# Keys and values through one wide product, and new places for tiles in SBUF, in a two-block transformer kernel

## The chip, the cores and the metric

The kernel runs on one core of one Trainium2 chip. The metric is the device time of one execution in microseconds (us); the kernel before takes 1009.96 us, the median of three runs (1009.23 to 1010.29). [...]

## The reference

The input is one sequence of 256 tokens with 1024 features, in fp32. The first block is a mixer with four branches (a short convolution, stick-breaking attention, an RWKV recurrence and a spatial gate), then a feed-forward with a short convolution. The second block has two layers; each has attention to a memory of 256 tokens, and a wide feed-forward. The change concerns the keys and values. Cut to that:

```python
def rmsnorm(x, g):
    y = x * lax.rsqrt(jnp.mean(x * x, axis=-1, keepdims=True) + EPS)
    return y * g

for l in range(2):
    if l == 1:                                   # layer 1: keys and values of the tokens
        kv = rmsnorm(h, kv_norm) @ w_kv          # (256, 1024) @ (1024, 512)
        k_shared = rmsnorm(kv[..., :256].reshape(B, S, 4, 64), k_norm)
        v_shared = kv[..., 256:].reshape(B, S, 4, 64)
    ...
    mkv = rmsnorm(mem, mem_norm[l]) @ w_mem_kv[l]   # both layers: keys and values of the memory
    mk = rmsnorm(mkv[..., :256].reshape(B, 256, 4, 64), mem_k_norm[l])
    mv = mkv[..., 256:].reshape(B, 256, 4, 64)
    mem_out = memory_attention(mqh, mk, mv)
    h = h + concat([main_out, mem_out]) @ w_out[l]
    h = h + square(relu(rmsnorm(h, norm_mlp[l]) @ w_up[l])) @ w_down[l]
```

There are thus three products for keys and values: the memory's for layer 0 and for layer 1, and the tokens' for layer 1. The keys are normalised head by head (4 heads of 64).

## The kernel before

All large products are done as three products of fp32r halves: each operand x is split into a high half h and a low half l, and `mm3` (L207) issues h·h, h·l and l·h into one accumulator in PSUM. A matmul here has a stationary operand (128 columns, loaded by LDWEIGHTS) and a moving operand (256 or 512 columns). A row `mm<-a,wh` of the profile names the output, then the moving and the stationary operand.

- `load_split` (L195) loads 512 KB of weights through SP's queue into a tile `raw`; ACT rounds it to `wh` (L203), DVE subtracts to get `wl` (L204). The tiles have four buffers each, of 1024 fp32 (4096 bytes a partition).
- `fm_part` (L254) gives an output with features on the partitions: weights stationary, activations moving, 256 columns (all tokens). `tm_part` (L262) gives an output with tokens on the partitions: activations stationary, 256 weight columns moving. Both are called narrow below. `wide_block` (L320) is as `tm_part`, with 512 weight columns moving, and is called wide. The up-projections of the last two feed-forwards (`fm_blocks`, L277) alternate: a matmul of 512 columns (both halves of the activation moving over `wh`), then one of 256 columns (the high half over `wl`).
- `tick()` steps generators that stand `beside` the main stream, so that small work (transposes, norms) comes between its pieces; `finish` runs one to its end. The scheduler then fixes each engine's order when the program is built; engines wait for each other by semaphores, and TensorE takes its matmuls in the order in which they stand.
- Keys before: `memory_keys` (L905), `memory_values` (L912) and L1441 to L1452 make keys features-first with `fm_part` and values tokens-first with `tm_part`, 48 narrow matmuls each. `scaled_keys` (L847) squares on ACT; `normed_keys` (L862) sums the squares by head with four fp32 matmuls of 2 columns (`head_sums`, `ssq`), takes the power -1/2 on GpSimd (`power`, L393), widens the factors on DVE (`rkx`, L440), spreads them over the features with four fp32 matmuls of 128 columns (`spread_heads`) and multiplies on DVE.
- Features of the first block's output for its feed-forward (`normalised_features`, L1095) are transposed beside `memory_values(1)`; the feed-forward's 22 up blocks follow (L1118).

Where tiles lie. The pools place tiles one after another, so a tile of a few bytes shifts what comes after it. In the built program, taking the byte at which the moving and the stationary operand start, modulo 256, the split matmuls stand so:

| split matmuls before | same remainder | stationary 64 further | moving 64 further | other |
|---|---|---|---|---|
| narrow, 2890 | 2624 | 48 (values of memory, layer 1) | 48 (keys of memory, layer 1) | 170 |
| wide, 2312 | 2096 | 24 (`yrw`) | 0 | 192 (`y`, both layers of block two) |

The 170 are the layer-0 memory products (96), the pool weights (42) and the band products (32).

Of the kernel before, what the change touches and what calls it, by code (L numbers as in the profile page):

```python
# [112 lines left out]
def build(tc, I, out):  # L113
# [345 lines left out]
    def load_const(p, key):  # L459
        t = p.tile([P, CARR[key].shape[1]], CDT[key], name=nm(key), tag=key)  # L460
# [33 lines left out]
    def mt(shape, name, dt=F32, tag=None, bufs=1):  # L494
        return m1.tile(shape, dt, name=nm(name), tag=tag or name, bufs=bufs)
# [351 lines left out]
    def scaled_keys(dst, z, gain, f):  # L847

        sq = scr([P, T], "ssq", f)
        S.activation(out=sq, in_=z, func=AF.Square)  # L850
        S.mul(dst, z, gain)
        return sq

# [8 lines left out]
    def normed_keys(dst, sq, f, m):  # L862

        yield
        r = scr([P, 4], "rk4", f)
        head_factor(r, head_sums(sq, f)[:, 0:4], m, f)
        yield
        wide = scr([P, 4, 64], "rkx", f)
        widen_heads(wide, r)
        yield  # L870
        tt(dst, dst, spread_heads(wide, 2, f))
# [33 lines left out]
    def memory_keys(l):  # L905
        o = halves(fm_block(I["w_mkv"][l, 0], hm[l]))
        return [scaled_keys(mkv[l][0][:, j], o[j], mem_gain[:, l : l + 1], "B") for j in range(2)]

    def memory_keys_norm(l, sqs):
        return together(*(normed_keys(mkv[l][0][:, j], sqs[j], "B", mmem) for j in range(2)))  # L910

    def memory_values(l):  # L912
        o = halves(tm_block(I["w_mkv"][l, 1], hm[l]))
        for j in range(2):
            S.mul(mkv[l][1][:, j], o[j], rmem[:, j : j + 1])
# [154 lines left out]
    ksq = memory_keys(0)  # L1070
    finish(mf)
    beside(memory_keys_norm(0, ksq))
# [10 lines left out]
    memory_values(0)  # L1083
    r = sums.mean()
    power(r)
    ksq = memory_keys(1)
    finish()
    xn = tok8()
    for j in range(2):
        late(S.mul(xn[:, j], x2[:, j], r[:, j : j + 1]))  # L1090
    xp = pair8()

    def normalised_features():
        yield from features(xn, range(KT), lambda k, z: split_scaled(xp[:, k], z, pvec("ffn_norm_g", k, k + 1)))

    nf = beside(normalised_features(), 0, 1.0)
    memory_values(1)
    finish(nf)
    beside(memory_keys_norm(1, ksq))
# [18 lines left out]
    for n in range(NFF):  # L1118
        o = halves(fm_block(I["w_up"][n], xp))
# [317 lines left out]
    snk = wa.tile([P, 12], F32, name="snk")  # L1437
    nc.gpsimd.dma_start(out=snk, in_=I["sinks"])
    kn = wa.tile([P, 2, T], F32, name="kn")
    mtok, rtok = wa.tile([P, 2], F32, name="mtok"), wa.tile([P, 2], F32, name="rtok")  # L1440
    o, vo = psum_mm(), psum_mm()  # L1441
    for a in (0, 4):
        if a:
            finish(tf)
            power(rtok, sums2.mean(mtok))
        fm_part(o, load_split(I["w_kv"][0][:, a : a + 4], 4), kvp[0], a, a + 4)
        tm_part(vo, load_split(I["w_kv"][1][:, a : a + 4], 4), kvp[0], a, a + 4)
    o, vo = halves(o), halves(vo)
# [138 lines left out]
```

## Time and profile before

| | |
|---|---|
| median of three runs | 1009.96 us |
| the profiled execution, its own time | 1010.36 us |
| its span on the chip | 1008.6 us |
| TensorE matmul busy | 998.1 us (99%) |
| VectorE, ScalarE, GpSimd busy | 690.8, 553.9, 142.1 us |
| DMA | 176.25 MB, 175 GB/s on average |

In the rows PE is TensorE (PEld its weight loads), DVE is VectorE, ACT is ScalarE, POOL is GpSimd. Matmuls are pipelined: the next one starts while the last still drains, so the durations of single matmuls add up to more than the span, and a group's "busy" counts a shared stretch once. What a matmul costs the stream is the distance from its start to the next one's start. "Mean ns" of a group is the duration of one, drain included.

### The profile page before, as it was taken

How to read it: one execution, taken by the hardware profiler on the slowest of the kernel's cores; microseconds unless marked ns; L12 is line 12 of the kernel's file. 1: busy time of each engine (PE TensorE's matmuls, PEld its weight loads, DVE VectorE, ACT ScalarE, POOL GpSimd, SP SyncE). 2: the span in 40 equal slices, each digit the busy share in tenths (PEclk: the TensorE clock that was granted, in tenths of full speed). 3: DMA queues.
4: the chain of work that ended last, by engine and by line, in shares of the span. 5: the costliest groups of instructions: out<-in, count | busy, mean ns of one | idle time of the engine just before them, and what ended most of it. 6: DMA issues, size and time to landing. Idle time of an engine off the chain costs nothing.

```text
span 1008.6 us, 16844 instructions
## 1 busy us (share of the span) xinstructions
PE 998.1 (99%) x6528; PEld 865.8 (86%) x6528; DVE 690.8 (68%) x1089; ACT 553.9 (55%) x965; POOL 142.1 (14%) x129
## 2 busy tenths in 40 slices
PE   9999999999999999999999999999999999999998
PEld 8999777788899999988987888888898668888886
DVE  6795477888558888855676777646468877776443
ACT  6754465365566655635665655535366466564331
POOL 0110001320000000001220344300021104443000
PEclk9999999999999999999999999999999999999999
DMA  8644533575466555555534555565562335555661
GB/s 285 226 148 136 177 116 114 162 250 192 169 209 195 182 180 188 188 188 187 174 123 145 188 184 188 186 196 187 189 226 88 105 104 182 188 185 189 197 209 64
DMA packets 50592, 176.25 MB, mean 175 GB/s; under 512 B 5776, under 2 KB 7056, under 8 KB 50128
## 3 DMA queue, kind: packets, MB, share of 16 engines
q1 hardware_dynamic: 50112, 174.38, 52.2%
q8 instruction: 51, 0.84, 0.3%
q10 hardware_dynamic: 288, 0.52, 0.1%
q0 software_dynamic: 112, 0.27, 0.1%
q14 instruction: 29, 0.24, 0.1%
HBM read 174.10 MB, written 1.05 MB: 174 GB/s over the span
## 4 chain that ended last, share of the span: by engine, by line
PE 91%; DVE 3%; ACT 2%; DMA 1%; issue 1%; SPq 0%; POOL 0%; ACTq 0%; DVEq 0%
PE mm L127 78%; PE ps L127 13%; DVE wl L204 1%; ACT wh L203 1%; DMA wlo<-in_lora 1%; DMA raw<-in_w_in 1%; DVE sc L360 0%; DVE mxs L1199 0%; DVE dd L363 0%; ACT uh L1349 0%; SPq L201 0%; ACT sc L1217 0%; DVE mxs L1205 0%; POOL var L393 0%; ACT sqw L409 0%
## 5 line engine op out<-in xcount | busy, mean ns | idle before, releaser
L204 DVE TENSOR_TENSOR wl<-raw,wh 128x1024 fp32r<-128x1024 f32 (+2 forms) x318 | 386.1, 1216 | 234.1 <-ACT wh L203 232.9
L203 ACT CAST wh<-raw 128x1024 fp32r<-128x1024 f32 (+2 forms) x318 | 328.4, 1034 | 349.1 <-PE mm L127 316.1
L127 PE MATMUL mm<-a,wh 128*128 128x256 f32 (+1 forms) x1520 | 363.6, 322 | 0.2 <-DVE a L363 0.2
L127 PE MATMUL mm<-a,wl 128*128 128x256 f32 x1008 | 283.9, 282 | 0.0
L127 PEld LDWEIGHTS mm<-a,wh 128*128 128x128 f32 x1520 | 252.9, 190 | 25.2 <-issue 0.7
L127 PEld LDWEIGHTS mm<-a,wl 128*128 128x128 f32 x1008 | 191.8, 190 | 0.1
L127 PE MATMUL mm<-wh,u 128*128 128x512 f32 x512 | 158.6, 389 | 0.0
L127 PE MATMUL mm<-wh,a 128*128 128x512 f32 (+1 forms) x512 | 144.7, 357 | 0.0
L127 PEld LDWEIGHTS mm<-wh,u 128*128 128x128 f32 x512 | 96.1, 188 | 20.1
L1274 POOL TENSOR_TENSOR u<-gate,u 128x256 fp32r<-128x256 f32 x64 | 84.4, 1320 | 160.0 <-ACT u L1273 160.0
L127 PEld LDWEIGHTS mm<-wh,a 128*128 128x128 f32 x512 | 90.8, 189 | 13.4 <-issue 0.3
L127 PE MATMUL mm<-wl,u 128*128 128x512 f32 x256 | 99.6, 389 | 0.0
L127 PE MATMUL mm<-wl,a 128*128 128x512 f32 (+1 forms) x256 | 89.7, 350 | 0.0
L127 PEld LDWEIGHTS mm<-wl,u 128*128 128x128 f32 x256 | 48.1, 188 | 9.7
L127 PE MATMUL mm<-wh,ff 128*128 128x512 f32 x176 | 54.9, 390 | 0.0
L127 PEld LDWEIGHTS mm<-wl,a 128*128 128x128 f32 x256 | 48.5, 189 | 5.4
L360 DVE SCALAR_TENSOR_TENSOR cv<-mm,pv,cv 128x255 f32<-128x255 f32 x88 | 42.2, 479 | 1.4
L127 PE MATMUL mm<-wh,y 128*128 128x512 f32 x112 | 38.6, 409 | 0.5 <-ACT y L352 0.5
L127 PEld LDWEIGHTS mm<-wh,ff 128*128 128x128 f32 x176 | 33.0, 188 | 6.8
L127 PE MATMUL mm<-wl,ff 128*128 128x512 f32 x88 | 34.3, 389 | 0.0
L360 DVE SCALAR_TENSOR_TENSOR gate<-gate 128x256 f32<-128x256 f32 x64 | 32.0, 502 | 2.0
L1149 POOL TENSOR_TENSOR a<-a,gfb 128x512 f32<-128x512 f32 x4 | 7.1, 1785 | 177.1 <-issue 149.8
(345 smaller groups left out, 1179.8 us busy)
## 6 DMA issues: line engine op xcount, KB each, us to landing
raw<-in_w_up SPq DMA_DIRECT2D x108, 512.0 KB, 3.6
raw<-in_w_dn SPq DMA_DIRECT2D x86, 512.0 KB, 3.3
raw<-in_w_in SPq DMA_DIRECT2D x36, 512.0 KB, 3.9
raw<-in_w_gate SPq DMA_DIRECT2D x32, 512.0 KB, 3.9
raw<-in_w_out SPq DMA_DIRECT2D x16, 512.0 KB, 3.8
raw<-in_outs SPq DMA_DIRECT2D x8, 512.0 KB, 4.0
raw<-in_w_mkv SPq DMA_DIRECT2D x8, 512.0 KB, 3.5
raw<-in_w_o SPq DMA_DIRECT2D x8, 512.0 KB, 4.2
```

The source lines that it names most:

```text
L127: ins = f(*a, **k)
L203: S.copy(wh[:, :m], raw[:, :m])
L204: V.tensor_tensor(out=wl[:, :m], in0=raw[:, :m], in1=wh[:, :m].bitcast(F32), op=ALU.subtract)
L360: return V.scalar_tensor_tensor(out=o, in0=a, scalar=sc, in1=b, op0=op0, op1=op1)
L1149: G.tensor_tensor(out=y3[:, j, c], in0=x3[:, j, c], in1=gfb[:, c], op=ALU.mult)
L1274: G.tensor_tensor(out=u.l[:, n], in0=sq, in1=u.h[:, n].bitcast(F32), op=ALU.subtract)
```

## The change

1. Keys and values come from one `wide_block` of 512 columns (256 of keys, 256 of values), tokens first, for all three products. `keys_values` copies the keys out of PSUM on ACT and scales the values there; DVE squares the keys and sums the squares by head (`tensor_reduce`). `normed_keys` forms the factor (DVE, GpSimd), multiplies on DVE, and TensorE transposes the normalised keys into features-first order (4 transposes for a product). The host packs the weights accordingly.
2. The first block's features are transposed in two parts: half of them beside the second memory product, half beside the start of the up blocks; the first two up blocks are done half by half (`up_blocks`).
3. Small tiles (`mt`, `load_const`, `snk`, `mtok`, `rtok`, `kss`) take whole lines of 256 bytes, and slots of `wh` and `wl` are 4352 bytes long instead of 4096.
4. In a slot, weights in pieces of fewer than 512 columns start 64 bytes in; wide ones start at 0.

| split matmuls after | same remainder mod 256 | stationary 64 further | moving 64 further |
|---|---|---|---|
| narrow, 2602 | 32 (band products) | 2330 | 240 |
| wide, 2456 | 1944 | 512 (up-projections of the last two feed-forwards) | 0 |

A slot is 17 × 256 bytes, so modulo 512 neighbouring slots differ by 256: of the wide matmuls with the same remainder modulo 256, half have the moving operand 256 bytes off modulo 512. Before, all 2096 agreed modulo 512.

```diff
     def load_split(src, kt, n=256, tag="w", bufs=4, size=1024, raw=None):
...
-        wh = wp.tile([P, size], F32R, name=nm("wh"), tag=tag + "h", bufs=bufs)
-        wl = wp.tile([P, size], F32R, name=nm("wl"), tag=tag + "l", bufs=bufs)
+        wh, wl = (wp.tile([P, size + 64], F32R, name=nm("w" + z), tag=tag + z, bufs=bufs) for z in "hl")
         m = kt * n
+        if n < 512:
+            wh, wl = wh[:, 16:], wl[:, 16:]
...
-    def wide_block(src, x, kt):
+    def wide_block(src, x, kt, half=None):
...
+            if half and a == kt // 2:
+                half()
...
     def load_const(p, key):
-        t = p.tile([P, CARR[key].shape[1]], CDT[key], name=nm(key), tag=key)
+        n = CARR[key].shape[1]
+        t = p.tile([P, (n + 63) // 64 * 64], CDT[key], name=nm(key), tag=key)[:, :n]
...
     def mt(shape, name, dt=F32, tag=None, bufs=1):
+        if shape[-1] < 64:
+            return m1.tile([P, 64], dt, name=nm(name), tag=tag or name, bufs=bufs)[:, : shape[-1]]
...
+    def keys_values(os_, mv, factor):
+        kz, ss = scr([P, 2 * T], "gate", bufs=4), scr([P, 8, 4], "kss", bufs=2)[:, :2]
+        for j, o in enumerate(os_):
+            with urgent():
+                S.copy(kz[:, j * T : j * T + T], o[:, :T])
+                S.mul(mv[:, j], o[:, T:], factor[:, j : j + 1])
+            sq = scr([P, T], "ssq", "B")
+            tt(sq, kz[:, j * T : j * T + T], kz[:, j * T : j * T + T])
+            V.tensor_reduce(out=ss[:, j], in_=sq.rearrange("p (h c) -> p h c", c=64), op=ALU.add, axis=AX.X)
+        return kz, ss
+
+    def normed_keys(dst, kz, ss, m, gain):
+        stt(ss, m.rearrange("p (a o) -> p a o", o=1).to_broadcast([P, 2, 4]), 64.0 * RMS_EPS, ss)
+        power(flat(ss))
+        for _ in range(2):
+            yield
+        heads = kz.rearrange("p (h c) -> p h c", c=64)
+        late(tt(heads, heads, flat(ss).rearrange("p (k o) -> p k o", o=1).to_broadcast([P, 8, 64])))
+        yield
+        o = psum("B")
+        for j in range(2):
+            for a in range(2):
+                TE.transpose(o[:, j * T + a * P : j * T + a * P + P], kz[:, a * T + j * P : a * T + j * P + P], ident)
+        S.mul(flat(dst), o, gain)
+        yield
...
+    def memory_kv(l):
+        kz, ss = keys_values(wide_block(I["w_mkv"][l], hm[l], KT), mkv[l][1], rmem)
+        return normed_keys(mkv[l][0], kz, ss, mmem, mem_gain[:, l : l + 1])
...
+    nf = beside(first_features(), 0, 1.0)
+    kf = memory_kv(1)
     finish()
...
+    beside(kf)
+    nf = beside(normalised_features(range(4, 8)), 0, 1.0)
...
+    def up_blocks():
+        os_ = [psum_mm(), psum_mm()]
+        for a in (0, 4):
+            if a:
+                finish(nf)
+            for n, o in enumerate(os_):
+                fm_part(o, load_split(I["w_up"][n][:, a : a + 4], 4), xp, a, a + 4)
+                if a:
+                    yield o
+        for n in range(2, NFF):
+            yield fm_block(I["w_up"][n], xp)
...
+    kz, ss = keys_values(wide_block(I["w_kv"], kvp[0], KT, ended), vt, rtok)
+    knf = beside(normed_keys(kn, kz, ss, mtok, swa_gain), 0, 1.0)
```

TensorE's order is the same in both programs up to the memory's first product. On TensorE at that place (`mem` the memory's split features, `mm` an accumulator, the row before it the end of the RWKV branch's output) stood before:

```order
L127 MATMUL ps_2714<-wl_2693,yrw_2357 128x512
L127 MATMUL ps_2714<-wh_2692,yrw_2358 128x512
L127 MATMUL mm_2724<-mem_2481,wh_2726 128x256
L127 MATMUL mm_2724<-mem_2483,wh_2726 128x256
L127 MATMUL mm_2724<-mem_2481,wl_2727 128x256
```

and on TensorE at the same place stands now:

```order
L127 MATMUL ps_2714<-wl_2693,yrw_2357 128x512
L127 MATMUL ps_2714<-wh_2692,yrw_2358 128x512
L127 MATMUL mm_2724<-wh_2727,mem_2481 128x512
L127 MATMUL mm_2724<-wl_2728,mem_2481 128x512
L127 MATMUL mm_2724<-wh_2727,mem_2483 128x512
```

Moving and stationary operand have changed places, and the moving one has 512 columns.

On TensorE after the tokens' keys and values, in layer 1 (`bq` the features of the query products that fill the time), the norm of the keys stood before as:

```order
L127 MATMUL mm_7846<-bq_6092,wl_7849 128x256
L127 MATMUL ps_7878<-cb_269,ssq_7836 128x2 x2
L127 MATMUL ps_7884<-cb_269,ssq_7839 128x2 x2
L127 MATMUL mm_7846<-bq_6092,wh_7890 128x256 x2
...
L127 MATMUL mm_7846<-bq_6092,wl_7891 128x256
L127 MATMUL ps_7923<-cb_269,rkx_7907 128x128 x2
L127 MATMUL ps_7927<-cb_269,rkx_7909 128x128 x2
L127 MATMUL mm_7939<-bq_6092,wh_7941 128x256 x2
```

and on TensorE there stands now (`gate` is the buffer of the keys), after 43 matmuls of the query product:

```order
L127 MATMUL mm_7684<-bq_5974,wl_7719 128x256
L127 MATMUL mm_7684<-bq_5974,wh_7718 128x256 x2
L127 MATMUL mm_7684<-bq_5974,wl_7719 128x256
L127 MATMUL ps_7748<-cb_269,gate_7671 128x128 x4
L127 MATMUL mm_7762<-bq_5974,wh_7764 128x256 x2
```

Eight fp32 matmuls have gone and four transposes have come.

On VectorE at the same place (`kss` the sums by head, `wl` the low half of weights to come), with what each waits for, stands now:

```order
L367 TENSOR_TENSOR ssq_7680<-gate_7671 128x256 [waits Activation_49]
L872 TENSOR_REDUCE kss_7672<-ssq_7675 128x4 [waits DVE_49]
L872 TENSOR_REDUCE kss_7672<-ssq_7680 128x4 [waits DVE_49]
L206 TENSOR_TENSOR wl_7807<-raw_7805,wh_7806 128x1024 [waits DMAHW5_49,PE_49,Activation_49]
L364 SCALAR_TENSOR_TENSOR kss_7672<-mtok,kss_7672 128x8 [waits DVE_49]
L367 TENSOR_TENSOR gate_7671<-gate_7671,kss_7672 128x512 [waits Pool_49]
L206 TENSOR_TENSOR wl_7910<-raw_7908,wh_7909 128x1024 [waits DMAHW6_49,PE_49,Activation_49]
```

A weight split stands between the sums and their use, and the multiplication waits for GpSimd with the next weight split behind it.

## Rows read from the trace of the kernel before

**Rows 1.** The page: TensorE's share, its granted clock, the chain of waits.
```profile
PE 998.1 (99%) x6528; PEld 865.8 (86%) x6528; DVE 690.8 (68%) x1089; ACT 553.9 (55%) x965; POOL 142.1 (14%) x129
...
PEclk9999999999999999999999999999999999999999
...
PE 91%; DVE 3%; ACT 2%; DMA 1%; issue 1%; SPq 0%; POOL 0%; ACTq 0%; DVEq 0%
```

**Rows 2.** TensorE's waits, longest of ten: engine, line, for whom, total, times, longest.
```profile
PE mm L127 <- DVE cold L485: 1.2, 1, 1.2
```

**Rows 3.** Groups by form, up blocks, 310 to 420 us: count, busy us, mean ns.
```profile
L127 PE MATMUL mm<-a,wh 128*128 128x256 f32 x613 | 110.4, 283 | 0.0
L127 PE MATMUL mm<-a,wl 128*128 128x256 f32 x306 | 86.6, 283 | 0.0
```

**Rows 4.** Groups by form, memory keys of layer 1, 281.5 to 286.5 us.
```profile
L127 PE MATMUL mm<-mem,wh 128*128 128x256 f32 x30 | 5.2, 276 | 0.0
```

**Rows 5.** Groups by form, memory values of layer 1, 287 to 290 us.
```profile
L127 PE MATMUL mm<-wh,mem 128*128 128x256 f32 x18 | 3.3, 281 | 0.0
```

**Rows 6.** Groups by form, the same product after four transposes, 290.9 to 291.6 us.
```profile
L127 PE MATMUL mm<-wh,mem 128*128 128x256 f32 x4 | 0.7, 277 | 0.0
```

**Rows 7.** Groups by form, up-projection of a last feed-forward, 570 to 640 us.
```profile
L127 PE MATMUL mm<-a,wh 128*128 128x512 f32 x199 | 70.4, 399 | 0.0
L127 PE MATMUL mm<-a,wl 128*128 128x256 f32 x198 | 55.6, 281 | 0.0
```

**Rows 8.** Groups by form, down-projection of the same, 645 to 680 us.
```profile
L127 PE MATMUL mm<-wh,u 128*128 128x512 f32 x104 | 32.2, 389 | 0.0
L127 PE MATMUL mm<-wl,u 128*128 128x512 f32 x52 | 20.2, 389 | 0.0
```

**Rows 9.** Groups by form, two branch outputs, 214.8 to 217.4 and 227.9 to 231.2 us.
```profile
L127 PE MATMUL ps<-wh,ysb 128*128 128x512 f32 x8 | 2.6, 389 | 0.0
...
L127 PE MATMUL ps<-wh,yrw 128*128 128x512 f32 x8 | 2.7, 395 | 0.0
```

**Rows 10.** Groups by form, whole span: the memory's four products.
```profile
L127 PE MATMUL mm<-wh,mem 128*128 128x256 f32 x64 | 12.0, 282 | 0.0
...
L127 PE MATMUL mm<-mem,wh 128*128 128x256 f32 x64 | 11.6, 282 | 0.0
```

**Rows 11.** TensorE's timeline, tokens' keys: start us, duration us, instruction, count.
```profile
735.23 0.28 PE L127 MATMUL mm<-wh,a 128*128 128x256 f32 x1
735.35 0.60 PE L127 MATMUL ps<-cb,a 128*128 128x128 f32 x4
735.71 0.36 PE L127 MATMUL mm<-wh,a 128*128 128x256 f32 x1
735.91 0.28 PE L127 MATMUL mm<-wl,a 128*128 128x256 f32 x1
...
746.11 0.95 PE L127 MATMUL ps<-cb,ssq 128*128 128x2 f32 x8
746.92 0.36 PE L127 MATMUL mm<-bq,wh 128*128 128x256 f32 x1
...
749.88 1.05 PE L127 MATMUL ps<-cb,rkx 128*128 128x128 f32 x8
750.69 0.48 PE L127 MATMUL mm<-bq,wh 128*128 128x256 f32 x2
```

**Rows 12.** Groups by form, VectorE and GpSimd, whole span: operations like the new norm's.
```profile
L204 DVE TENSOR_TENSOR wl<-raw,wh 128x1024 fp32r<-128x1024 f32 x308 | 380.6, 1237 | 232.3 <-ACT wh L203 231.1 <-issue 0.3
...
L1205 DVE TENSOR_REDUCE mxs<-sc 128x2 f32<-128x256 f32 x6 | 2.5, 411 | 0.0
...
L363 DVE TENSOR_TENSOR yt<-yt,var 128x512 f32<-128x512 f32 x1 | 0.7, 693 | 1.8 <-POOL var L393 1.8
...
L393 POOL TENSOR_TENSOR var<-var,mhalf 128x8 f32<-128x8 f32 x1 | 1.7, 1667 | 9.9 <-DVE var L369 9.9
```

More of the change, by code (lines that the diff above doesn't have):

```diff
@@ L844, in gated_output @@
             tick()
[L847 to L852, printed above, removed]
     def head_factor(r, sums, m, f):
@@ L860, in head_factor @@
         power(r)
-    def normed_keys(dst, sq, f, m):
-        yield
-        r = scr([P, 4], "rk4", f)
-        head_factor(r, head_sums(sq, f)[:, 0:4], m, f)
+    def keys_values(os_, mv, factor):
[15 more added lines that the diff above has]
+        late(tt(heads, heads, flat(ss).rearrange("p (k o) -> p k o", o=1).to_broadcast([P, 8, 64])))
+        yield
+        o = psum("B")
[3 more added lines that the diff above has]
+        S.mul(flat(dst), o, gain)
         yield
[L868 to L871, printed above, removed]
     mem_gain = cp.tile([P, 2], F32, name="mem_gain")
@@ L903, in memory @@
             yield
[L905 to L915, printed above, removed]
+    def memory_kv(l):
+        kz, ss = keys_values(wide_block(I["w_mkv"][l], hm[l], KT), mkv[l][1], rmem)
+        return normed_keys(mkv[l][0], kz, ss, mmem, mem_gain[:, l : l + 1])
     rw = beside(rwkv(), 0, 0.65)
@@ L1069, in build @@
     mf = beside(features(merged, range(KT), lambda k, z: split(mp[:, k], z)), 0, 1.0)
-    ksq = memory_keys(0)
+    kf = memory_kv(0)
     finish(mf)
-    beside(memory_keys_norm(0, ksq))
+    beside(kf)
     x2 = tok8()
@@ L1082, in build, with normalised_features, first_features @@
             sums.add(z, j, cb)
-    memory_values(0)
     r = sums.mean()
     power(r)
-    ksq = memory_keys(1)
-    finish()
[L1088 to L1099, printed above, removed]
+    xn = tok8()
+    xp = pair8()
+    def normalised_features(ks):
+        yield from features(xn, ks, lambda k, z: split_scaled(xp[:, k], z, pvec("ffn_norm_g", k, k + 1)))
+    def first_features():
+        yield
+        yield
+        for j in range(2):
+            late(S.mul(xn[:, j], x2[:, j], r[:, j : j + 1]))
+        yield
+        yield
+        yield from normalised_features(range(4))
+    nf = beside(first_features(), 0, 1.0)
+    kf = memory_kv(1)
+    finish()
+    beside(kf)
+    nf = beside(normalised_features(range(4, 8)), 0, 1.0)
     ph1.close()
@@ L1116, in conv3 @@
         return a
-    for n in range(NFF):
-        o = halves(fm_block(I["w_up"][n], xp))
+    def up_blocks():
[9 more added lines that the diff above has]
+            yield fm_block(I["w_up"][n], xp)
+    for n, o in enumerate(up_blocks()):
+        o = halves(o)
         ga, va = conv3(o[0], n), conv3(o[1], NFF + n)
@@ L1436, in build, with ended @@
     CS = load_const(wa, "cs")
-    snk = wa.tile([P, 12], F32, name="snk")
+    snk = wa.tile([P, 64], F32, name="snk")[:, :12]
     nc.gpsimd.dma_start(out=snk, in_=I["sinks"])
     kn = wa.tile([P, 2, T], F32, name="kn")
[L1440 to L1448, printed above, removed]
-    ksq = [scaled_keys(kn[:, j], o[j], swa_gain, "B") for j in range(2)]
-    vt = wa.tile([P, 2, 256], F32, name="vt")
-    for j in range(2):
-        S.mul(vt[:, j], vo[j], rtok[:, j : j + 1])
-    knf = beside(together(*(normed_keys(kn[:, j], ksq[j], "B", mtok) for j in range(2))), 0, 1.0)
+    mtok, rtok = (wa.tile([P, 64], F32, name=n)[:, :2] for n in ("mtok", "rtok"))
+    vt = wa.tile([P, 2, 256], F32, name="vt")
+    def ended():
+        finish(tf)
+        power(rtok, sums2.mean(mtok))
+    kz, ss = keys_values(wide_block(I["w_kv"], kvp[0], KT, ended), vt, rtok)
+    knf = beside(normed_keys(kn, kz, ss, mtok, swa_gain), 0, 1.0)
     y = pair8(wa, "y")
@@ L1531, in _host_arrays @@
     A["w_out2"] = np.stack([blocks(i["w_out_2"][0], 512), blocks(pairs(i["w_out_2"][1], 0), 512)])
-    A["w_mkv"] = np.stack([blocks(i["w_mem_kv_2"][l]) for l in range(2)])
-    A["w_kv"] = blocks(i["w_kv_2"])
+    A["w_mkv"] = np.stack([blocks(i["w_mem_kv_2"][l], 512)[0] for l in range(2)])
+    A["w_kv"] = blocks(i["w_kv_2"], 512)[0]
     A["w_up2"] = np.stack([blocks(i["w_up_2"][l]) for l in range(2)])
```

## The prediction

> **What bounds the kernel now.** I read the page first: TensorE is busy for 99% of the span, at the full granted clock in all forty slices, and 91% of the chain of waits is TensorE's own [rows 1]. Then its waits: ten in the whole execution, the longest 1.2 us, before the first product [rows 2]. So the time is the length of TensorE's stream, and an edit is worth what it takes out of that stream or what wait it puts in. Third, the groups by form, to see what one matmul costs the stream. In the up blocks 919 narrow matmuls fill 110 us (two or three of the 919 had begun before): 120 ns from start to start, for a duration of 283 ns [rows 3]. In the down-projection 156 wide ones fill 35 us: 227 ns, for 389 ns [rows 8]. Both differences are about 163 ns, so in an undisturbed stretch start to start is the duration less 163. This gives the finding on which most of the sum rests: one shape has several prices. A narrow matmul takes 120 ns in the up blocks, 113 in the memory keys of layer 1 [rows 4], 118 in the values that follow [rows 5], and 114 in the same product once transposes have interrupted it [rows 6]. A wide one takes 226 ns over `ysb` and 232 over `yrw` [rows 9]. The clock is the same everywhere; what differs by the table of places is where the two operands start: same remainder modulo 256 at 120, moving 64 bytes further at 113, stationary 64 further at 118 or 114. Wide ones are the other way round: 226 or 227 with the same remainder, 232 with the stationary 64 further.
>
> **The change, part by part.** All terms are against the profiled execution's own 1010.36 us (span 1008.6 and 1.8 around it), which is 0.4 above the median of the three runs.
>
> *Narrow, weights stationary.* Of the 2330 narrow matmuls that get the stationary operand 64 further, 512 belong to the up-projections below and 42 are pool weights that had another relation already; 1776 go from the 120 ns relation to that of rows 5 and 6. If they settle at 118 the gain is 1776 × 2 = 3.6 us; at 113, as in rows 4, 1776 × 7 = 12.4 us. Rows 5 and 6 are one product at one relation in two states, and no row says which state a long stretch keeps. So I take the middle, 115.5 ns: 1776 × 4.5 = 8.0 us. A loss I exclude: no narrow group at any other relation is slower than 283 ns, and the memory's products, transposes among them, have 282 [rows 10]. Nothing stays possible if the place isn't the cause.
>
> *Narrow, weights moving.* 240 get the moving operand 64 further, the relation of rows 4: 240 × 7 = 1.7 us.
>
> *The up-projections of the last two feed-forwards.* Now 198 pairs (512 columns, then 256) fill 70 us: 353.5 ns a pair [rows 7]. With the stationary operand 64 further the nearest rows are 232 ns for the wide part (`yrw`, rows 9) and 113 to 118 for the narrow one: about 347.5, a gain of 6 ns for each of 512 pairs, 3.1 us. Ends: nothing, and 227 + 113 = 340, which gives 6.9 us.
>
> *Wide over `y` and `yrw`.* 216 of them come to the same remainder: 6 ns each [rows 9], 1.3 us; the low end is nothing.
>
> *One wide product for keys and values.* 288 narrow matmuls become 144 wide ones. Before, 96 took 120 ns; the other 192 took 113 to 119 by rows 4 to 6 and 10, say 118: 11.5 + 22.7 = 34.2 us. After: 144 × 227 = 32.7 us [rows 8]. Gain 1.5 us. [...]
>
> *The norm of the keys.* `ssq` takes 0.81 us from its start to the next product's, `rkx` likewise; the matmul that follows is 0.08 longer than one in the stream [rows 11]. That is 0.89 × 2 for each of three products: 5.3 us, all on TensorE. Four transposes take 0.36 us and lengthen the next matmul's distance from 0.12 to 0.20: 0.44 × 3 = 1.3 us. Gain 4.0 us.
>
> *A new wait.* In layer 1 the transposes of the keys stand behind 43 narrow matmuls, 43 × 0.116 = 5.0 us after the product's end. The chain to them, from like operations [rows 12] and estimates for the rest: the copy out of PSUM and the squares are done about 1.1 us after the end, two sums of 0.41, the weight split queued in front (1.24), the factor 0.2, the power on GpSimd 1.67, the multiplication 0.69: 5.7 us. So TensorE waits about 0.8 us there; 0 to 2.5 as ACT's and DVE's queues have it. VectorE's next weight split stands behind the multiplication, which waits for GpSimd; the weights have four buffers, so it may come 2 us late without a wait on TensorE. After the two memory products 42 wide matmuls (9.5 us) or 84 narrow ones cover the same chain.
>
> *At nothing:* the split of the features into halves, since the same transposes stay in the stream, and 18 wide matmuls (4.1 us) stand between the first half's last transposes and their first use; padding of small tiles other than by the places; copies and squares on ACT and DVE, busy 55% and 68% [rows 1]. Without that cover each is a wait below 1 us.
>
> The sum: 8.0 + 1.7 + 3.1 + 1.3 + 1.5 + 4.0 - 0.8 = 18.8 us; 1010.36 - 18.8 = 991.6, and 0.4 less against the median: about 991 us. With all high ends (12.4, 1.7, 6.9, 1.3, 1.5, 4.0, no wait) 27.8: 982. With the low ends (3.6, 1.7, 0, 0, 1.5, 4.0, less 2.5) 8.3: 1001.
>
> **Rivals.**
>
> *The places do nothing.* The differences in rows 3 to 6 could come from what ran beside them. For it: the stretches are short, 5 and 3 us against 110, and rows 5 and 6 show two prices for one relation. Against it: the up blocks hold 283 ns over 919 matmuls whatever runs beside, and the layer-1 keys hold 276 over a whole product. Then 1.5 + 4.0 - 0.8 = 4.7 us are left: 1005 us. [...]
>
> *The period is 512, and wide ones pay (slower).* Every same-remainder wide matmul before agreed modulo 512 as well. With slots of 4352 bytes half of the 1944 wide ones, 972, get operands 256 bytes apart modulo 512. If that costs them what `yrw` pays, 6 ns, it is 5.8 us; if it costs what the narrow relation costs relative to its best, twice 7 ns, 13.6 us. If then the narrow ones gain nothing, since half of them are at a relation that no row shows, the sum is 4.7 - 5.8 to 4.7 - 13.6, about -5: 1015 us. It decides from 4.8 ns for each such matmul on. For it: no row has two relations 256 apart. Against it: slices of one weight tile start at multiples of 512 bytes and up to four different ones show the same price, which says only that the period is not longer than 512.
>
> *The norm's chain is late.* If the wait comes at its upper end at all three products, 7.5 us instead of 0.8 go back: 998 us. For it: the multiplication sits on VectorE behind a weight split and GpSimd's power. Against it: the cover after the memory products is twice the chain.
>
> **How the numbers follow.** The forecast (places matter, chain mostly covered) gets 0.78, at 991, its own range 982 to 1001. Places do nothing: 0.08, 1005. The slower rival: 0.06, 1015. The late chain: 0.06, 998. Parts of several: 0.02. The range 982 to 1003 holds the forecast, the late chain and the border to the first rival. Under 0.2% (2 us) a measurement of this kernel can't tell a change from none; faster holds the forecast, the first rival and the late chain: 0.91; the same 0.03; slower 0.06.
>
> **What would show it.** In the up blocks the narrow group's mean duration goes from 283 to 276 to 281 ns; 283 refutes the largest term. In the up-projections the pair falls below 353 ns. The down-projection stays at 389 ns; about 395 in every other weight tile is the slower rival. `ssq` and `rkx` are gone from TensorE, with 12 transposes of `gate` in their place, and a wait of TensorE for VectorE's `gate` of 0 to 2.5 us stands after the tokens' keys. The stretch before the memory's first product has TensorE's order unchanged, so what it gains is from places alone: at the prices taken, some 480 weight-stationary and 96 weight-moving narrow matmuls, 2.8 us. The prediction is wrong if that stretch keeps its length, or if waits of several us come after the keys.

## The result and the profile after

The kernel after takes 1002.42 us, the median of five runs (1001.26 to 1005.57); the kernel before, beside it, 1009.47 us. The ratio is 0.9929, 95% interval 0.9916 to 0.9941: 7.1 us are gained where 18.8 were forecast. The profiled execution took 1003.33 us, its span is 1001.5 us.

On the page after, the busy line of the engines, the granted clock by slices, and the chain of waits by engine:

```profile
PE 989.3 (99%) x6348; PEld 850.6 (85%) x6348; DVE 692.8 (69%) x1089; ACT 554.3 (55%) x962; POOL 143.9 (14%) x126
...
PEclk9999999999999999999999999999999999999999
...
PE 86%; DVE 4%; ACT 3%; DMA 2%; issue 2%; POOL 1%; SPq 0%; ACTq 0%; DVEq 0%; POOLq 0%
```

TensorE still sets the end [rows 1], but 5% of the chain have gone from it to waits. TensorE's waits of after that before did not have, or had shorter (engine, line, for whom; total, times, longest):

```profile
PE ps L127 <- DMA wlo<-in_lora: 1.8, 1, 1.8
PE ps L127 <- DVE sc L371: 1.3, 2, 1.0
...
PE ps L127 <- DVE gate L367: 0.4, 1, 0.4
```

The last is the wait for the keys that was forecast. The first was not thought of: `wlo`, the low-rank weights of the RWKV branch, was waited for 0.6 us before.

Groups by form of after, as [rows 3, 7, 8, 9]: up blocks (310 to 418 us), up-projection (566 to 636), down-projection (645 to 680), the `yrw` output (228.4 to 231.2):

```profile
L127 PE MATMUL mm<-a,wh 128*128 128x256 f32 x613 | 108.4, 281 | 0.0
...
L127 PE MATMUL mm<-a,wh 128*128 128x512 f32 x199 | 70.4, 397 | 0.0
L127 PE MATMUL mm<-a,wl 128*128 128x256 f32 x199 | 55.9, 281 | 0.0
...
L127 PE MATMUL mm<-wh,u 128*128 128x512 f32 x104 | 32.2, 389 | 0.0
...
L127 PE MATMUL ps<-wh,yrw 128*128 128x512 f32 x8 | 2.6, 389 | 0.0
```

Narrow matmuls went from 283 to 281 ns, that is from 120 to 118 from start to start, and stay there for more than 900. The pairs of the up-projections are where they were: 70 us hold 199 of them, before 70 us held 198 [rows 7]; start to start the mean pair is 353.3 ns in both. The down-projection keeps 389 [rows 8]; `yrw` fell from 395 to 389 [rows 9].

From the starts of the first matmul of each stretch on TensorE, in us, with the differences from before in one profile each (the kernels in the later columns are told of below; in two of them, no shift and k/v only, the granted clock fell to 0.50 some 12 us into the span, which costs 1.7 us of their first row):

| stretch | before | after | no shift | shift only | k/v only | k/v, `kss` in lines | load and entries |
|---|---|---|---|---|---|---|---|
| start to the memory's first product | 244.76 | +0.23 | +0.30 | -1.33 | +1.47 | +0.31 | -3.27 |
| memory's products and `w_o` | 49.36 | -2.49 | -2.48 | +0.53 | -2.13 | -2.11 | -2.48 |
| up blocks | 129.41 | -2.84 | -0.65 | -2.37 | -0.76 | -0.77 | -6.09 |
| their down-projection | 60.83 | -0.02 | -0.02 | 0.00 | +1.65 | -0.02 | -0.02 |
| two last up-projections | 183.18 | 0.00 | -0.01 | 0.00 | 0.00 | -0.06 | -2.73 |
| two last down-projections | 179.16 | +0.10 | 0.00 | +0.08 | +5.00 | +0.06 | +0.04 |
| tokens' keys, values, norm | 21.59 | -1.44 | -1.40 | -0.44 | -1.38 | -1.39 | -1.44 |
| the rest | 140.25 | -0.64 | -0.49 | -0.29 | -0.28 | -0.01 | -0.67 |

The gain of after sits in the memory's products, the up blocks and the tokens' keys. Part 2 of the change has no run of its own; at the first two up blocks, which it rearranges, the distances between starts that are longer than the stretch's own add up to 1.0 us in after and to 0.5 in before (transposes and the matmul behind them left out). The first quarter of the span, for which 2.8 us were forecast, is 0.23 longer. Windows there, of after (length; busy time and instructions of the five engines; granted clock; DMA share; GB/s):

```profile
38.00:40.00 2.00, 0.23 (x3) 0.22 (x4) 2.00 (x3) 0.61 (x1) 0.00 (x0) 1.00 0.34 104
40.00:42.00 2.00, 2.00 (x10) 0.92 (x8) 1.30 (x2) 0.00 (x0) 0.00 (x0) 0.74 0.80 258
42.00:44.00 2.00, 2.00 (x8) 1.53 (x7) 1.10 (x2) 1.61 (x5) 0.00 (x0) 0.50 0.74 256
44.00:48.00 4.00, 4.00 (x35) 4.00 (x35) 2.59 (x5) 3.26 (x6) 0.00 (x0) 0.95 0.28 109
```

and two of the same windows of before:

```profile
38.00:40.00 2.00, 1.40 (x12) 1.20 (x10) 2.00 (x3) 1.65 (x2) 0.00 (x0) 1.00 0.31 82
...
42.00:44.00 2.00, 2.00 (x17) 1.95 (x16) 1.42 (x3) 1.96 (x6) 0.00 (x0) 1.00 0.74 268
```

In after TensorE stands for 1.8 of the 2 us from 38 on, and right behind it the granted clock is 0.74 and then 0.50: 8 matmuls run where 17 did. The three windows lose 2 x 0.26 + 2 x 0.50 + 4 x 0.05 = 1.7 us of full clock. With 1.2 us more of waiting this is 2.9 us, about what the places were to bring there.

The keys of layer 1 in after, on TensorE, then GpSimd, then VectorE (start, duration, instruction, idle before and for whom):

```profile
742.81 0.28 PE L127 MATMUL mm<-bq,wl 128*128 128x256 f32 x1
743.48 0.63 PE L127 MATMUL ps<-cb,gate 128*128 128x128 f32 x4 [0.39 <-DVE gate L367]
743.86 0.49 PE L127 MATMUL mm<-bq,wh 128*128 128x256 f32 x2
```

```profile
740.96 1.64 POOL L397 TENSOR_TENSOR kss<-kss,mhalf 128x8 f32<-128x8 f32 x1 [1.36 <-DVE kss L364]
```

```profile
742.64 0.69 DVE L367 TENSOR_TENSOR gate<-gate,kss 128x512 f32<-128x512 f32 x1 [1.76 <-POOL kss L397]
```

The power (1.64), the multiplication (0.69) and the transposes (0.38 to the next product) are as the prediction took them from [rows 11, 12]; the wait is 0.39 against 0.8.

### The profile page after: what moved, and what is told of

It is laid out like the page before. It is cut to its first block, busy times and chain, and to the rows that moved or that the text cites. A ratio compares the mean times of both kernels' runs of the same rounds, so it can differ in the third digit from the quotient of the medians.

```text
span 1001.5 us, 16469 instructions
## 1 busy us (share of the span) xinstructions
PE 989.3 (99%) x6348; PEld 850.6 (85%) x6348; DVE 692.8 (69%) x1089; ACT 554.3 (55%) x962; POOL 143.9 (14%) x126
## 4 chain that ended last, share of the span: by engine, by line
PE 86%; DVE 4%; ACT 3%; DMA 2%; issue 2%; POOL 1%; SPq 0%; ACTq 0%; DVEq 0%; POOLq 0%
PE mm L127 75%; PE ps L127 11%; DVE wl L206 2%; DMA raw<-in_w_in 2%; ACT wh L205 2%; DMA wlo<-in_lora 1%; POOL kss L397 0%; DVE a L361 0%; ACT sqw L413 0%; DVE sc L364 0%; DVE mxs L1227 0%; DVE dd L367 0%; ACT uh L1377 0%; SPq L203 0%; ACT sc L1245 0%
## 5 line engine op out<-in xcount | busy, mean ns | idle before, releaser
L127 PE MATMUL mm<-a,wh 128*128 128x256 f32 (+1 forms) x1488 | 354.4, 321 | 0.4 <-DVE a L367 0.2
L127 PE MATMUL mm<-a,wl 128*128 128x256 f32 x992 | 278.5, 281 | 0.0
L127 PEld LDWEIGHTS mm<-a,wh 128*128 128x128 f32 x1488 | 246.5, 189 | 25.4 <-issue 0.7
L127 PEld LDWEIGHTS mm<-a,wl 128*128 128x128 f32 x992 | 186.5, 188 | 0.1
L127 PE MATMUL mm<-wh,a 128*128 128x512 f32 (+1 forms) x512 | 148.1, 363 | 0.0
L127 PEld LDWEIGHTS mm<-wh,a 128*128 128x128 f32 x512 | 91.0, 188 | 14.7 <-issue 0.3
```

The source lines that it names most:

```text
L127: ins = f(*a, **k)
```

## The experiments

Times are medians; ratios are to the kernel before on the same chip, with 95% intervals.

**Which part brings what.** Two kernels, after without part 4 and before with part 4 alone. The first:

```diff
-        if n < 512:
-            wh, wl = wh[:, 16:], wl[:, 16:]
```

> The changed kernel without part 4: narrow weights start at 0 of their slots again, slots and small tiles stay. Theory A (the relation of the two operands modulo 256 sets the price): the narrow group of the up blocks goes back from 281 to 283 ns, start to start from 118 to 120; 1800 narrow matmuls x 2 ns = 3.6 us slower than the changed kernel, about 1006 us where that has 1002.4. Up-projection pairs stay at 353 ns. Rival B (the places do nothing, the gain is all from the wide product and the new norm): as the changed kernel, 1002.4.

Measured: 1005.16 us (1004.01 to 1005.63), ratio 0.9941 (0.9924 to 0.9957). Its up blocks from 310 to 418 us:

```profile
L127 PE MATMUL mm<-a,wh 128*128 128x256 f32 x602 | 108.4, 283 | 0.0
```

Narrow matmuls are back at 283 ns, and the up blocks 2.2 us longer than after's; all other stretches are as after's within 0.2. So the shift is the cause of the 2 ns, and what is left without it is 4.8 us in the trace. In the stretch before the memory the likeness is chance. Its 480 narrow matmuls with the weights stationary take 119.7 ns here and 115.5 on average in after, 2.0 us in all; but TensorE does not wait for `wlo` here, and instead the clock falls earlier, behind a wait of 1.2 us for `wh`:

```profile
12.00:14.00 2.00, 2.00 (x14) 2.00 (x13) 1.49 (x4) 1.97 (x4) 0.00 (x0) 0.66 0.99 371
14.00:16.00 2.00, 2.00 (x11) 2.00 (x11) 2.00 (x5) 1.86 (x5) 0.00 (x0) 0.50 1.05 370
```

The second, on the kernel before:

```diff
-        wh = wp.tile([P, size], F32R, name=nm("wh"), tag=tag + "h", bufs=bufs)
-        wl = wp.tile([P, size], F32R, name=nm("wl"), tag=tag + "l", bufs=bufs)
+        wh, wl = (wp.tile([P, size + 64], F32R, name=nm("w" + z), tag=tag + z, bufs=bufs) for z in "hl")
...
+        if n < 512:
+            wh, wl = wh[:, 16:], wl[:, 16:]
```

> The kernel before with part 4 and the longer slots alone. Theory A: the up blocks fall to 118 ns start to start, 1850 narrow matmuls gain 2 ns each: 3.7 us, 1005.8 us against 1009.5; the memory products of layer 1 change their relation and may lose what they had (113 ns). Rival B: no change, 1009.5. If the wait for wlo (1.8 us) and the fall of the clock behind it in the changed kernel come from the weights' places, they show here too and take back up to 3 us.

Measured: 1007.36 us (1006.39 to 1009.03), ratio 0.9967 (0.9954 to 0.998). The up blocks get 2.4 us shorter, the up-projections keep their length; the memory's second product gets 0.5 longer, since its keys leave the places of [rows 4] (119.6 ns instead of 113.4) and its values theirs. The wait for `wlo` is 1.2 us here and the clock stays at 1.00: the stretch before the memory gains 1.3.

**Keys and values alone.** After with neither part 3 nor part 4, and the tile of the sums by head at its own size (the last edit is shown):

```diff
...
-        kz, ss = scr([P, 2 * T], "gate", bufs=4), scr([P, 8, 4], "kss", bufs=2)[:, :2]
+        kz, ss = scr([P, 2 * T], "gate", bufs=4), scr([P, 2, 4], "kss", bufs=2)
```

> The changed kernel with the wide keys and values, the new norm and the split of the features, but with slots and small tiles as before. Theory A: 1.5 (wide product) + 4.0 (norm) - 0.8 (wait): about 1004.7 us against 1009.5, and narrow ones stay at 120 ns. Rival B: all of the gain, 1002.4. Rival C (the new norm's chain costs what it saves): 1008 or more.

Measured: 1013.23 us (1011.68 to 1013.9), ratio 1.0021 (1.001 to 1.0032): slower. The gains at the keys are there, but three down-projections got 1.7, 2.5 and 2.5 us longer (the rest of the loss, 1.5 us in the stretch before the memory, comes with the fall of the clock named above). Two buffers of 32 bytes move all that lies behind them by 64, `u` and `ff` among it, which are the stationary operands of those products. The same kernel with whole lines for this one tile:

```diff
-        kz, ss = scr([P, 2 * T], "gate", bufs=4), scr([P, 2, 4], "kss", bufs=2)
+        kz, ss = scr([P, 2 * T], "gate", bufs=4), scr([P, 8, 4], "kss", bufs=2)[:, :2]
```

> The kernel with only the wide keys and values, with one more edit: the two small tiles of the sums (kss) take 128 bytes each instead of 32, so that what lies behind them starts 256 bytes further on than in the kernel before and not 64. Theory A2: the moving weights and the stationary activations of the three down-projections have the same remainder again, 227 ns; the 6.6 us that these lost come back: about 1006.5 us where that kernel had 1013.2 and the kernel before 1010.6. Rival C (the new chain itself costs time): stays near 1013.

Measured: 1006.42 us (1005.8 to 1006.84), ratio 0.9963 (0.9951 to 0.9976). The down-projection from 655 to 690 us, first without, then with the lines:

```profile
L127 PE MATMUL mm<-wh,u 128*128 128x512 f32 x101 | 31.8, 396 | 0.0
```

```profile
L127 PE MATMUL mm<-wh,u 128*128 128x512 f32 x102 | 32.0, 391 | 0.0
```

(391 with a few transposes in the stretch; the matmuls over `wl` have 395 and 389.) No instruction on the engines and no order differs, and the three down-projections differ by 6.6 us: small tiles of 32 bytes cost more than the new product and norm give. (The medians differ by 6.8 us, on two chips; by the ratios it is 5.9.) The merged product and the norm by themselves are then worth 2.1 + 0.8 + 1.4 = 4.3 us by the table.

**What the places cost.** After with the weights of twenty up blocks, of the up-projections' third to sixteenth source and of the last down-projections at places 0, 16, 32, ..., 240, 8, 136, 192, 128 bytes further, in this order:

```diff
+SWEEP = (0, 4, 8, 12, 16, 20, 24, 28, 32, 36, 40, 44, 48, 52, 56, 60, 2, 34, 48, 32)
...
-            yield fm_block(I["w_up"][n], xp)
+            yield fm_block(I["w_up"][n], xp, SWEEP[n - 2])
...
```

> The changed kernel; each of 20 up blocks, each source of the last two up-projections from the third on and each load of the last two down-projections has its weights at another byte of the slot: 0, 16, 32, ... 240, then 8, 136, 192, 128. Theory A: the price follows the place: narrow 120 ns at 0 and between 113 and 118 elsewhere, the pair of the up-projections between 340 and 353, wide 227 at 0 and 231 to 236 elsewhere. Rival D (a stretch keeps the state that it entered with, whatever the place): the up blocks stay at one price over all places. Rival B: 118 everywhere.

One run, 1005.54 us. Start to start, in ns, means of 48 narrow, of 32 matmuls in pairs (half of 512, half of 256 columns), and of 12 wide ones:

| bytes further | 0 | 16 | 32 | 48 | 64 | 96 | 128 | 192 | 240 |
|---|---|---|---|---|---|---|---|---|---|
| narrow | 120.0 | 118.4 | 118.4 | 117.8 | 113.3 | 118.8 | 118.6 | 113.3 | 119.8 |
| pairs, per matmul | 176.8 | 173.7 | 173.5 | 173.5 | 176.5 | 173.7 | 175.6 | 176.7 | |
| wide | 227.5 | 231.2 | 233.6 | 232.8 | 229.8 | 234.2 | 233.1 | 233.3 | 227.4 |

Pairs are the mean over both up-projections, each block from its first start to the next block's. Wide ones want the same remainder (227.5) or 16 bytes less (227.4). But here 64 costs a narrow one 113.3, and in after 118. From 322.6 to 327.6 us (48 bytes) and from 328.4 to 333.1 us (64 bytes):

```profile
L128 PE MATMUL mm<-a,wh 128*128 128x256 f32 x30 | 5.3, 281 | 0.0
...
L128 PE MATMUL mm<-a,wh 128*128 128x256 f32 x28 | 4.8, 276 | 0.0
```

**192 instead of 64, and 32 for the up-projections.** Two kernels on after:

```diff
-            wh, wl = wh[:, 16:], wl[:, 16:]
+            wh, wl = wh[:, 48:], wl[:, 48:]
```

> The changed kernel with narrow weights 192 bytes into their slots instead of 64. Theory A2 (each place has its own price, and at 64 a stretch can settle at 113 or at 118 ns): at 192 the sweep's two blocks had 113.3 ns, so the up blocks' 1056 matmuls gain 4.7 ns each, 5.0 us, and with all 2016 narrow ones 9.5 us: about 993 us where the changed kernel has 1002.4. Up-projection pairs stay at 353 ns. Rival D (the state is what the entry into the stretch left, and 192 had it from its neighbours in the sweep): stretches stay at 118, 1002.

Measured: 1001.32 us (997.52 to 1002.83), ratio 0.9908 (0.9886 to 0.993). The up blocks took 126.5 us, as after's. With the up-projections' pieces at 32 bytes as well:

```diff
...
-                w = load_split(src[:, a : a + 4], 4)
+                w = load_split(src[:, a : a + 4], 4, off=8)
```

> As the run before, and the weights of the last two up-projections 32 bytes into their slots. Theory A2: in the sweep a matmul of these took 3.5 ns less at 32 than at 0 on average over 512 and 256 columns; 1024 of them, 3.6 us more: about 989.5 us. Rival D: no further gain, since the pair keeps the 353 ns that it entered with.

Measured: 1000.87 us (996.79 to 1002.37), ratio 0.9903 (0.9879 to 0.9926). The pairs took 353.4 ns; at the same 32 bytes in the run with sixteen places they had taken 346.9 (2 x 173.5), 6.6 less than at 0. (The 3.5 per matmul that was expected is about this difference.) So 64 or 192 has no one price for narrow ones, nor 32 for pairs.

**How the stream comes to a place.** One up block at 48 bytes in after, then all at 64:

```diff
...
-            yield fm_block(I["w_up"][n], xp)
+            yield fm_block(I["w_up"][n], xp, 12 if n == 2 else 16)
```

> The changed kernel, with the third up block alone at 48 bytes; all others stay at 64. Tells whether 64 has two states that a stretch keeps. Theory A2: the 19 blocks behind it come out of it in the state of 113 ns, as the block at 64 did in the sweep: 912 x 4.7 ns = 4.3 us, about 998 us. Rival E (64 costs 118 in a long stretch, and the sweep's block was too short to show it): the blocks go back to 118 within some tens of matmuls, 1002.

Measured: 998.91 us (997.23 to 1003.24), ratio 0.9896 (0.9871 to 0.9921); in the profile the 912 matmuls behind the block kept 117.8 ns (group mean 281). A block at 48 alone does not do it. In this profile the wait for `wlo` was 1.7 us, and the clock fell behind it to 0.66 and 0.50, as in after. Then the whole way that the run with sixteen places took to 64, once, and 64 from there on:

```diff
...
-            yield fm_block(I["w_up"][n], xp)
+            yield fm_block(I["w_up"][n], xp, {2: 0, 3: 4, 4: 8, 5: 12}.get(n, 16))
```

> The kernel after, with the weights of the third to sixth up block 0, 16, 32 and 48 bytes further in their slots, in this order, and all later ones 64 further. Open is why narrow matmuls with the stationary operand 64 further took 113.3 ns in one block of the run with sixteen places, right behind blocks at 0, 16, 32 and 48, and 118 where all blocks are at 64. Theory (how the stream enters the place sets which of two rhythms it keeps): the 768 narrow matmuls from the seventh up block on take 113 ns, the up blocks get about 3.5 us shorter than after (126.6 to 123), the time is about 999. Rival (the weights that ACT and DVE write beside it, for the next block, must lie elsewhere): the seventh block at most is at 113, all later ones at 118, the time 1002 to 1003.

Measured: 998.74 us (998.34 to 999.94), ratio 0.9891 (0.9876 to 0.9907). From 327 to 413 us:

```profile
L127 PE MATMUL mm<-a,wh 128*128 128x256 f32 x507 | 86.3, 276 | 0.0
L127 PE MATMUL mm<-a,wl 128*128 128x256 f32 x254 | 70.1, 276 | 0.0
```

All 768 matmuls at 64 bytes take 113.3 ns, in the place and beside the writes where after takes 118. The up blocks are 3.4 us shorter than after's. So the rival is wrong, and 113 can be kept for 768 matmuls. That the four blocks brought it, as the theory has it, this trace does not show: ahead of them, behind the transposes at 302.3 us, the stream was already near 115. It is shown where the stream stood at 118 ahead of them: in the run with sixteen places and in the last kernel below. Directly ahead of the block at 0, in this kernel (303.1 to 304.0 us) and in the last one (300.8 to 301.7):

```profile
L127 PE MATMUL mm<-a,wh 128*128 128x256 f32 x7 | 1.3, 277 | 0.0
...
L127 PE MATMUL mm<-a,wh 128*128 128x256 f32 x7 | 1.3, 281 | 0.0
```

Ten blocks alternating between 64 and 80, then ten between 48 and 64:

```diff
+ENTER = 5 * (16, 20) + 5 * (12, 16)
...
+            yield fm_block(I["w_up"][n], xp, ENTER[n - 2])
```

> The kernel after, with the places of the up blocks' weights alternating: ten blocks at 64, 80, 64, 80, ..., then ten at 48, 64, 48, 64, ... Theory (the entry sets the rhythm, and 48 before 64 is the right one): 64 blocks in the second half take 113 ns, those in the first half 118. Rival 1 (what is written beside must lie elsewhere): 64 blocks take 113 in both halves. Rival 2 (neither): 118 in both.

One run, 1000.14 us. The blocks at 80 took 118.7 to 118.9 ns, those at 48 117.8, and every block at 64 113.3 to 113.6, in both halves: by the letter the first rival's outcome, and the theory's 118 in the first half is wrong. But the run before, with 64 written beside 64, excludes that rival, and the trace shows another beginning: already the first block at 64, ahead of any other place, stood at 113. In this run, one block on either side of four transposes of the layer-1 keys (299.7 to 302.2 and 303.2 to 309 us):

```profile
L128 PE MATMUL mm<-a,wh 128*128 128x256 f32 x16 | 2.9, 281 | 0.0
...
L128 PE MATMUL mm<-a,wh 128*128 128x256 f32 x35 | 6.1, 276 | 0.0
```

The same transposes, at the same place of the order, left after's stream at 281. There it had been at 276 shortly before, and lost it between these two windows (296.2 to 298.6 and 300.9 to 303.3 us), where TensorE waits for weights:

```profile
L127 PE MATMUL mm<-a,wh 128*128 128x256 f32 x16 | 2.8, 276 | 0.0
...
L127 PE MATMUL mm<-a,wh 128*128 128x256 f32 x16 | 2.9, 281 | 0.0
```

The program does not decide it. Up to the up blocks after, the kernel with the entry and those with sixteen places, one block at 48 and alternating places have the same TensorE order and the same places; yet the 64 narrow matmuls from 30.5 us on took 113.3 ns in after and 117.8 in the other four. After (31.5 to 37.0 us), then the kernel with the entry (31.8 to 37.0):

```profile
L127 PE MATMUL mm<-a,wh 128*128 128x256 f32 x34 | 5.8, 276 | 0.0
...
L127 PE MATMUL mm<-a,wh 128*128 128x256 f32 x31 | 5.6, 281 | 0.0
```

So the rhythm is set where something interrupts the stream, transposes or a wait, and can come out either way, from one execution to another. It is then kept, also through other places: 113 came back nine times behind blocks at 80 and 48, and 118 stayed behind the block at 48 of the run with one such block, which had begun at 118. Without an interruption, at 64 bytes, only the way over 0, 16, 32 and 48 led from 118 to 113.

**The load of `wlo`.** After, with this load ahead of the two first blocks' shifts:

```diff
     z_first.update((b, fm_block(I["w_in"][6 + b], xp)) for b in (0, 2))
+    wlo = q2("wlo", "A")
+    nc.sync.dma_start(out=wlo, in_=I["lora"])
     finish()
...
-    wlo = q2("wlo", "A")
-    nc.sync.dma_start(out=wlo, in_=I["lora"])
```

> The kernel after, with one load moved: the 256 KB of low-rank weights (wlo) go out on SP right behind the first 16 weight pieces, some 20 us earlier, instead of behind two loads of 256 KB for the gate. The scheduler then puts the six low-rank products ten matmuls earlier on TensorE. Theory (the new wait and the clock that falls behind it cost the first stretch what the places give): the wait of TensorE for wlo (1.8 us in the profile after) is gone or below 0.5 us, the granted clock stays at 1.00 from 38 to 48 us (0.50 to 0.95 in the profile after), and the time is 1.5 to 4 us below the kernel after: about 999.5, with less spread between runs. Rival (another wait stands right behind it: the sigmoid and tanh on ACT, ready 36.7 us into the span): the time stays at 1002 and the wait is put down to ACT.

Measured: 997.07 us (995.79 to 1001.84), ratio 0.9878 (0.9857 to 0.9899), below after's interval. Windows of its profile, which is of its longest run:

```profile
10.00:15.00 5.00, 4.35 (x22) 4.15 (x23) 3.86 (x8) 4.20 (x9) 0.00 (x0) 0.68 1.04 378
```

```profile
40.00:42.00 2.00, 2.00 (x17) 1.75 (x14) 1.31 (x3) 1.70 (x5) 0.00 (x0) 1.00 0.79 264
42.00:44.00 2.00, 2.00 (x19) 2.00 (x18) 1.97 (x4) 2.00 (x4) 0.00 (x0) 1.00 0.61 223
```

The gain at the medians, 5.3 us, is more than the 1.5 to 4 expected. The wait is gone (0.2 us for ACT's `th` are left), and the clock is full where after's had fallen. In this run it fell elsewhere, in the first loads, to 0.68 over 5 us (1.6 us lost); no trace shows a run at the median, so where its 5.3 us come from is not shown. The spread did not get less: that expectation failed.

**Both together.** Early load, the up blocks' entry, and an entry for the pairs (third source at 0, fourth at 16, all later at 32 bytes):

```diff
...
-        for src in srcs[2:]:
+        for i, src in enumerate(srcs[2:]):
...
-                w = load_split(src[:, a : a + 4], 4)
+                w = load_split(src[:, a : a + 4], 4, off=min(4 * i, 8))
```

> The kernel after with the early load of wlo and the up blocks' entry over 0, 16, 32 and 48, and in the up-projections of the last two feed-forwards the third source at 0, the fourth at 16, all later ones at 32 bytes. Theory (the entry sets the rhythm of the pairs as well): the pairs from the fifth source on take 350 to 351 ns, as the block at 32 in the run with sixteen places, against 353; each up-projection gets 0.6 to 1.0 us shorter (after: 91.3 and 91.9), and with the wait gone (3 to 5 us by the run with the early load) and the up blocks at 113 (3.4 us) the time is about 992. Rival (the pairs keep 353 at 32, as in the run with 192 and 32): the up-projections keep their length and the time is about 993.5; the rival below that (wait and entry do not add up): 996 or more.

Measured: 994.35 us (993.75 to 995.5), ratio 0.9845 (0.9831 to 0.9859). Page, then the pairs from 563 to 628 us:

```profile
PE 980.7 (99%) x6348; PEld 844.9 (85%) x6348; DVE 692.7 (70%) x1089; ACT 556.2 (56%) x962; POOL 143.6 (14%) x126
```

```profile
L127 PE MATMUL mm<-a,wh 128*128 128x512 f32 x189 | 65.6, 392 | 0.0
L127 PE MATMUL mm<-a,wl 128*128 128x256 f32 x188 | 52.6, 280 | 0.0
```

The pair takes 346.7 ns (229 + 118) against 353.4 at the same 32 bytes without the entry, as in the run with sixteen places. Each up-projection is 1.4 us shorter; the expected 0.6 to 1.0 rested on 350 to 351 for that place. The up blocks, which the stream entered at 118, are 3.3 us shorter than after's. The stretch before the memory is 3.5 us shorter than after's, with the clock at 1.00 throughout. TensorE's busy time is 8.6 us below after's. This version beats both kernels.

## Why the prediction was wrong

*The step that failed* is the size of the largest term: "Rows 5 and 6 are one product at one relation in two states, and no row says which state a long stretch keeps. So I take the middle, 115.5 ns". The mechanism (the place sets the price) was right: without the shift the price is 120 again. But the middle of two states is no state. In after's profile the longest stretch, 970 matmuls in the up blocks, stood at 118, and the 1056 matmuls there gave 2.2 us, where the middle gives them 4.8. Shorter stretches stood at 113.3: 92 matmuls from 14.7 us, 64 from 30.5 us. So the 480 before the memory came to 115.5 on average, the middle by luck, and gave 2.0. With some 0.6 us from the other 240 the term is worth about 5 us instead of 8.0, an estimate from the distances between starts in the profiles of after and of the kernel without the shift. What [rows 5, 6] show, one product at 118 and then at 114 behind transposes, was the mechanism itself; the prediction saw the two states and did not ask what sets them. Two more steps failed by as much: the pairs and the wait, below.

*Narrow, weights moving*: the same mistake, one state taken for the price. Nearly all of them took 118 too, not the 113 of [rows 4]; 0.5 us instead of 1.7.

*The up-projections' pairs*: 3.1 us forecast, 0.0 measured. The wide part was priced from 24 matmuls over `yrw`, the narrow part by the 113 to 118 of another order of matmuls; as a pair they came out at 235 + 118 = 353. No row had this order of matmuls at another place. The forecast 347.5 is reached, but only with an entry (346.7).

*Wide over `y` and `yrw`*: `yrw` fell from 395 to 389 as forecast; the two outputs over `y` gained 0.4 us together, of 1.3 for both.

*One wide product, the norm, the new wait*: 1.5 + 4.0 - 0.8 = 4.7 forecast; 4.3 measured with keys and values alone. The wait was 0.39 and stood where it was forecast. As a sum these steps were right; product and norm were not measured apart, and at the first up blocks, which the split of the features rearranges, TensorE's waits got 0.5 us longer where the prediction put nothing.

*Not in the sum*: the longer wait for `wlo` and the clock behind it, 2.9 us. The prediction took the stretch before the memory as a test of the places alone, because it "has TensorE's order unchanged". By its own sign ("if that stretch keeps its length") it is wrong there, but not because the places do nothing: its waits changed. [rows 2] has the longest alone, and the 0.6 us for a load issued behind two others of 256 KB was passed over. TensorE comes earlier when its matmuls are shorter; the load hardly does (issued at 33.09 us in after, at 33.40 in before).

*The whole*: 2.2 (up blocks) + 4.6 (products and norms, from the table: 2.49 + 0.65 + 1.44) + 0.6 (the rest) - 0.2 (start) - 0.1 = 7.1. Of the 11.7 us that are missing, about 3 are the largest term's, 3.1 the pairs', 2.9 the wait's and the clock's, 1.2 those of the narrow matmuls with weights moving and 0.7 those over `y` and `yrw`. The measured 1002.42 lies inside the range of 982 to 1003, close to its end; the forecast's own low end is 1001.7 by its sum (1009.96 - 8.3), not 1001.

*The rivals.* "The places do nothing" is refuted, though its 1005 is nearer than 991: the runs without the shift, and the 6.6 us of the small tiles, show that places do much. In the run with the shift alone places moved one shape, the keys of the memory's second product, from 113.4 to 119.6 ns. "The period is 512" is refuted: half of after's wide matmuls are 256 bytes off modulo 512, and the down-projection keeps 389 [rows 8]. The late chain did not come: 0.39 us.

*Open.* What the rhythm is made of is not shown: only that it has two values at one place, that it is kept through hundreds of matmuls and changes of the weight tile, and what changed it here. Nor is the spread settled. After's kind of kernel differs by 4.6 us between runs even where the mean clock is 1.0 (996.79, 1000.32 and 1001.43 with 192 and 32 bytes); both kernels with the up blocks' entry keep within 1.8 us. 1056 matmuls at 113 instead of 118 would be 4.9 us, and the profiles show that an interruption comes out either way in one and the same program; so some of the runs without a profile may have kept the faster rhythm in the up blocks. No trace of them shows it. It would also explain why the early load gained 5.3 us at the medians, and the same load 3.5 in the trace of the last kernel. And why the clock falls in some executions and not in others is open: its fall costs 1.7 us each time.

## What to carry to other kernels

If one shape shows two prices in a trace, ask which of them the longest stretch holds, and forecast that stretch by the one state or the other, each with a chance, and not by the middle; then look at what interrupts the stream ahead of it. When a stream of matmuls gets shorter, list the loads that it waits for already, however briefly, because they need not get earlier with it (here `wlo`, issued at 33.09 us instead of 33.40 and waited for 1.8 us instead of 0.6). A small tile that is added ahead of others can change the price of products behind it (here two of 32 bytes made three down-projections 6.6 us longer): compare the places of all operands first, not only those that the change names.

## What the runs showed of the hardware

- A narrow matmul of one shape, on one clock, took 113.3, 118 or 120.0 ns from start to start; two of the three at one place of the operands, each held for hundreds in a row (768 and 970). Transposes (group mean 281 to 277 ns [rows 5, 6]), a wait for weights (276 to 281 in after, between 298.6 and 300.9 us), or weights at other places (281 at 48 bytes to 276 at 64, in the run with sixteen places) changed the one into the other, and one and the same stretch of a program stood at 113.3 in one execution and at 117.8 in four others.
- Pairs of a wide and a narrow matmul took 353.4 or 346.7 ns at one place (32 bytes), by the way in which the stream had come to it.
- A wide one took 227 ns with both operands at the same remainder modulo 256, or the weights 16 bytes before it, and 230 to 234 at the other places of the table.
- Behind a wait for `wlo` of 1.5, 1.7 and 1.8 us, in three kernels, TensorE's granted clock fell to 0.50; behind waits of 0.6 to 1.4 us at the same place, and behind one of 1.6 (alternating places), it stayed at 1.00. In five other profiles (no shift, k/v only, 192, 192 and 32, early load) it fell to 0.50 some 12 us into the span, behind waits of 1.2 to 1.7 us for `wh`; behind 1.2 us there in the last kernel it did not. The length of a wait does not decide it alone. Each of the eight falls cost 1.7 us of full clock (in k/v only, from 10 to 15 us, 5 x 0.34).
